# RWKV preparation: seven kinds of store to DRAM issued from POOL's queue instead of SP's and ACT's

## The chip, the core and the metric

The kernel runs on one core of a Trainium2 chip. The core has five engines, each working through its own list of instructions in order: PE (TensorE, matmuls), DVE (VectorE), ACT (ScalarE), POOL (GpSimd) and SP (SyncE). SP computes nothing: it only issues transfers. ACT and POOL can issue transfers too. An issue takes its place in the engine's own list, so an issue that has to wait holds up whatever stands behind it on that engine. The bytes are moved by 16 DMA engines, whichever engine issued the transfer.

The metric is device time in microseconds (us). Lower is better. Three runs of the kernel before gave a median of 2121.01 us.

## What is computed

The program is one block of a model over 512 latent tokens and 256 context tokens with 1024 channels: a token mixer with two branches (RWKV-7 and Mamba-2) and a mixture of 16 experts behind it. The change lies in the preparation of the RWKV branch, whose recurrence reads:

```python
def step(s, inp):
    r_t, w_t, k_t, v_t, kk_t, a_t = inp
    sa = jnp.einsum('bhvk,bhk->bhv', s, -kk_t)
    s = s * w_t[:, :, None, :] + sa[..., None] * (kk_t * a_t)[:, :, None, :] + v_t[..., None] * k_t[:, :, None, :]
    return s, (jnp.einsum('bhvk,bhk->bhv', s, r_t) if with_output else None)
s, ys = lax.scan(step, s0, seq, reverse=reverse)
```

It runs over 768 tokens, once forward and once backward, for 16 heads of 64 channels. All arithmetic is in float32.

## The kernel before

**The recurrence in chunks.** The 768 tokens are cut into 12 chunks of 64. Within a chunk the steps are solved at once, which needs products of the operands within the chunk and the inverse of a triangular 64x64 matrix. Only from chunk to chunk does a serial scan remain. All that the scan needs is made in a preparation stage, written to DRAM in the layout that the scan wants, and loaded again by `scan_load`.

**The preparation (`rw_all`).** It goes over 8 pairs of heads (p = 0 to 7) and two directions (d = 0 forward, 1 backward): 16 products, from about 100 to 640 us of the span. The pieces that matter here are these.

- `split_w` (L280 to L286) loads a weight block `wraw` of 512 KB on SP (L280), rounds it on ACT to `whi` (L283) and takes the rest on DVE to `wlo` (L286). PE projects the tokens with both (L311, L314). This input projection is the filler: between the small matmuls of the preparation PE works off its matmuls. `wraw` and `wlo` share three buffers.
- `rw_head` loads two small weights `lwr` (L609), rounds them on ACT (L612), and turns `v` into `VT` (L622, L623).
- `rw_elem` makes the operands `AR` and `BK` from exponentials; ACT evacuates its matmuls `ra`, `rac` into `s` and `a` (L660, L661).
- `rw_products` multiplies them on PE (`pab`, L735, L738), DVE masks the results into two tiles `X` (L741), and six stores per product put parts of X into `d1` (L748, four) and `d3` (L750, two): these are the operands of the inverses, 48 KB each in pieces of 128 bytes. Four more stores, from POOL, put X into `ALd` and `RBd` (L751, L752). Then PE transposes BK three times (`pbt`, L760), ACT copies each result to `BT` (L762; two buffers), and each BT is stored to `BTd` (L763, 256 KB). The third BT of a product needs the buffer of the first, so it waits until the first one's store has landed.
- `tri` loads `Ad` from `d1` (L778), builds 32x32 inverses on DVE (L783 to L805) and stores them twice, `Tf` and its transpose `Tt`, to `d2` (L809, L810).
- `tri2` loads them as `T11` and `TT` (L824, L821), joins them with `A21` (L826, from `d3`) into 64x64 inverses by PE (`px`, `py`, L835, L845) and ACT (L838, L848), and stores them to `TTd` (L852, two per pair). The last three pairs' `tri2` run beside the first scan.

**What sets the order.** PE's list stands as written in the code. DVE, ACT, POOL and SP are ordered by the framework's scheduler, which simulates the program when it is built. The same framework gives every transfer one of eight completion counters: the transfers of SP and ACT share eight (DMAHW0 to 7), those of POOL have another eight (DMASW0 to 7). In this program a transfer that takes a counter first waits until the transfer that had it before has landed.

**Queues before.** SP issues all loads, the stores to `d1`, `d3`, `d2` and `TTd`; ACT issues the stores to `BTd` and, at the end of the preparation, the loads of the first scan step (`scan_first`: `sAR`, `sBK`); POOL issues the stores to `ALd`, `RTd`, `RBd`, `VTd`, `bond`, `zd`.

Of the kernel before, what the change touches and what calls it, by code (L numbers as in the profile page):

```python
# [86 lines left out]
class Block:  # L87
# [629 lines left out]
    def rw_products(self, pool, ps, p, d, AR, BK, f, t2, last=False):  # L717

        nc = self.nc
        H = [slice(0, 64), slice(64, 128)]  # L720
        V = [H[1], H[0]]
        chunk = lambda s: s if d == 0 else (3 - s if s < 4 else 15 - s)
        al = AR.rearrange("q (g u) t -> q g (u t)", u=2)
        ALd, RTd, RBd = (x[p // 2][:, p % 2] for x in (self.ALd, self.RTd, self.RBd))
        for a in range(2):
            nc.gpsimd.dma_start(ALd[:, H[d], d, a].rearrange("g k t -> k g t"), al[H[a], 0:6])
            nc.gpsimd.dma_start(RTd[:, H[d], a].rearrange("g k t -> k g t"), al[H[a], 6:10])
        Xs = [pool.tile([128, 20, 64], F32, name="X", tag="X", bufs=2) for _ in range(2)]
        for u0, m in ((0, 1), (4, 2), (8, 2)):
            pa = [ps.tile([128, 4, m, 64], F32, name="pab", tag="ra") for _ in range(2)]  # L730
            for u in range(4):
                for a in range(2):
                    w = BK[H[a], chunk(u0 + u)].rearrange("p x t -> p (x t)")
                    if m > 1:
                        nc.tensor.matmul(pa[a][:, u], w, AR[H[a], u0 + u:u0 + u + 9:8, :], start=True, stop=True)  # L735
                    else:
                        for h in range(2):
                            nc.tensor.matmul(pa[a][H[h], u, 0], w[:, H[h]], AR[H[a], u, :], start=True, stop=True)  # L738
            for a, X in enumerate(Xs):
                o = X[:, 4:20].rearrange("p (x u) t -> p u x t", x=2)[:, u0 - 4:u0] if m > 1 else X[:, 0:4, None]  # L740
                nc.vector.tensor_mul(o, pa[a], self.mk[:, d, None, 0:m].to_broadcast([128, 4, m, 64]))  # L741
            f()
            f()
        for a, X in enumerate(Xs):
            xs = X.rearrange("q (g u) t -> q g (u t)", u=2)
            for b in range(2):
                q = 2 * d + b
                nc.sync.dma_start(self.d1[p % 3][:, 24 * q + 12 * a:24 * q + 12 * a + 12, :],  # L748
                                  X[32 * q:32 * q + 32, 0:12, 32 * b:32 * b + 32])
            nc.sync.dma_start(self.d3[p % 3][d, :, 12 * a:12 * a + 12], X[64 * d:64 * d + 32, 0:12, 32:64])  # L750
            nc.gpsimd.dma_start(ALd[:, V[d], d, a].rearrange("g k t -> k g t"), xs[V[d], 0:6])  # L751
            nc.gpsimd.dma_start(RBd[:, :, d, a].rearrange("g k t -> k g t"), xs[:, 6:10])  # L752
            next(t2, None)
        if last:
            self.first = self.scan_first()

        for g in range(3):
            pt = ps.tile([128, 4, 128], F32, name="pbt", tag="ra")
            for u in range(4):
                nc.tensor.transpose(pt[:, u], BK[:, chunk(4 * g + u)].rearrange("p x t -> p (x t)"), self.ident)  # L760
            BT = pool.tile([128, 4, 128], F32, name="BT", tag="BT", bufs=2)
            nc.scalar.activation(BT, pt, AF.Copy)  # L762
            nc.scalar.dma_start(self.BTd[p // 2][2 * g:2 * g + 2, p % 2, :, d].rearrange("g k u c -> k g (u c)"),  # L763
                                BT.rearrange("k (g u) c -> k g (u c)", u=2))
            f()
            next(t2, None)

    def tri(self, pool, p):

        nc = self.nc
        d1, d2 = self.d1[p % 3], self.d2[p % 2]
        T, Tf = self.T, self.Tf
        Ad = pool.tile([96, 3, 16, 16], F32, name="Ad", tag="Ad", bufs=2)
        lo, hi = slice(0, 16), slice(16, 32)
        for i, (x, y) in enumerate(((lo, lo), (hi, hi), (lo, hi))):
            nc.sync.dma_start(Ad[:, i], d1[x, :, y].rearrange("s u t -> u s t"))  # L778
        prod = lambda n: pool.tile([96, 512], F32, name="pr", tag="pr", bufs=PRB)[:, :n]
        for s in range(14, -1, -1):  # L780
            n, r = 15 - s, slice(s + 1, 16)
            prv = prod(2 * n * n).rearrange("p (h c t) -> p h c t", h=2, t=n)
            nc.vector.tensor_mul(prv, T[:, :, r, r], Ad[:, 0:2, s, r][:, :, None, :].to_broadcast([96, 2, n, n]))  # L783
            nc.vector.reduce_sum(T[:, :, r, s], prv, axis=AX.X)
            if s % 2 == 0:
                yield
        Tt = pool.tile([96, 32, 32], F32, name="Tt", tag="Tt", bufs=1)
        U, W = (Tt.rearrange("p a b -> p (a b)")[:, i:i + 256].rearrange("p (s x) -> p s x", x=16) for i in (0, 256))
        nc.scalar.activation(U, T[:, 0].rearrange("p x s -> p s x"), AF.Copy)
        nc.scalar.activation(Tf[:, 0:16, 0:16], T[:, 0], AF.Copy)  # L790
        nc.scalar.activation(Tf[:, 16:32, 16:32], T[:, 1], AF.Copy)
        for c in range(0, 16, 2):
            n = c + 2
            prv = prod(32 * n).rearrange("p (c s t) -> p c s t", c=2, s=16)
            nc.vector.tensor_mul(prv, T[:, 1, c:c + 2, 0:n][:, :, None, :].to_broadcast([96, 2, 16, n]),
                                 Ad[:, 2, :, 0:n][:, None].to_broadcast([96, 2, 16, n]))
            nc.vector.reduce_sum(W[:, c:c + 2], prv, axis=AX.X)
            if c % 4:
                yield
        for s in range(0, 16, 2):  # L800
            n = 16 - s
            prv = prod(32 * n).rearrange("p (c s x) -> p c s x", c=16, s=2)
            nc.vector.tensor_mul(prv, W[:, :, s:16][:, :, None, :].to_broadcast([96, 16, 2, n]),
                                 U[:, s:s + 2, s:16][:, None].to_broadcast([96, 16, 2, n]))
            nc.vector.reduce_sum(Tf[:, 16:32, s:s + 2], prv, axis=AX.X)  # L805
            if s % 4:
                yield
        nc.scalar.activation(Tt.rearrange("p c t -> p t c"), Tf, AF.Copy)
        nc.sync.dma_start(d2[:, 0], Tf)  # L809
        nc.sync.dma_start(d2[:, 1], Tt)  # L810

    def tri2(self, pool, ps, tag, p):

        nc = self.nc
        d2, d3 = self.d2[p % 2], self.d3[p % 3]
# [3 lines left out]
        for q in range(4):  # L819
            d, b = divmod(q, 2)  # L820
# [28 lines left out]
            if tag == "A":  # L849
                yield  # L850
        for a in range(2):
            nc.sync.dma_start(self.TTd[p // 2][:, p % 2, :, a].rearrange("g k t -> k g t"),  # L852
                              TT[:, 12 * a:12 * a + 12].rearrange("q (g u) t -> q g (u t)", u=2))
        yield

# [1267 lines left out]
```

## Time and profile before

| | us |
|---|---|
| median of three runs | 2121.01 |
| lowest and highest of the three | 2115.63, 2121.77 |
| the profiled execution | 2122.66 |
| its span (first to last instruction) | 2120.9 |
| PE busy in the span | 1865.1 |
| DVE busy in the span | 1245.5 |
| ACT busy in the span | 838.0 |
| POOL busy in the span | 256.3 |

The profile is of a fourth execution. The span is the time that its traced instructions cover; 1.8 us of the execution's own time lie around it. Busy time is summed over the whole span, which has stages with different limits, so a share of it says little on one stage: the preparation has to be read by itself.

### The profile page before, as it was taken

The page shows a single profiled execution, that of the slowest core. Times are in us where ns is not written, and L with a number is a line of the kernel's source. Part 1 is how long each engine was busy: PE and PEld are TensorE (multiplying, and loading weights), DVE is VectorE, ACT ScalarE, POOL GpSimd, SP SyncE. Part 2 cuts the span into 40 slices and gives each one's busy share as a digit, 9 for nine tenths or more (in the row PEclk, how much of TensorE's full clock was granted, in tenths as well). Part 3 has the DMA queues.
Part 4 walks back from the last instruction along what each step waited for, and adds up shares of the span by engine and source line. Part 5 has one row for each costly group of instructions (what it writes and reads, how often), then busy time and mean ns, then how long its engine had stood idle before and what let it go on. Part 6 is the DMA issues. An engine that isn't in the chain of part 4 may idle for free.

```text
span 2120.9 us, 34560 instructions
## 1 busy us (share of the span) xinstructions
PE 1865.1 (88%) x13683; PEld 1251.7 (59%) x13696; DVE 1245.5 (59%) x2240; ACT 838.0 (40%) x1344; POOL 256.3 (12%) x383
## 2 busy tenths in 40 slices
PE   5989788888778988998997997788999999999997
PEld 2867676676656755656675664467878444434332
DVE  4467888987878667545563888875355111324315
ACT  5445555555534344343535443354334112212113
POOL 1123333232320000000000000000001000000002
PEclk8989989999888999999998999789999999999999
DMA  6357686777779676976536334257766899999997
GB/s 240 90 129 173 154 201 180 184 169 192 182 196 241 213 244 196 288 238 188 176 119 207 122 125 136 100 185 259 256 219 255 335 409 409 409 409 409 403 409 290
DMA packets 388414, 495.13 MB, mean 233 GB/s; under 512 B 138521, under 2 KB 278031, under 8 KB 385179
## 3 DMA queue, kind: packets, MB, share of 16 engines
q1 hardware_dynamic: 349883, 407.33, 57.6%
q0 software_dynamic: 21504, 68.70, 11.1%
q10 hardware_dynamic: 16864, 16.88, 2.5%
q8 instruction: 108, 1.77, 0.3%
q14 instruction: 55, 0.45, 0.1%
HBM read 393.96 MB, written 97.98 MB: 232 GB/s over the span
## 4 chain that ended last, share of the span: by engine, by line
PE 50%; DVE 18%; DMA 17%; ACT 7%; issue 6%; SPq 1%; POOL 1%; ACTq 0%; POOLq 0%; DVEq 0%
PE pl L311 9%; PE ph L1713 6%; DMA ew<-in_exp_w_dram 5%; DMA wraw<-in_w_in_dram 5%; PE pch L901 4%; PE pye L1800 4%; PE mp L1361 4%; PE pc L314 3%; DVE wlo L286 2%; PE pl L1314 2%; PE sps L1180 1%; PE py L901 1%; DMA BTd<-BT 1%; PE adaps L167 1%; PE ph L1714 1%
## 5 line engine op out<-in xcount | busy, mean ns | idle before, releaser
L311 PE MATMUL pl<-hlH,whi 128*128 128x512 f32 x672 | 246.3, 446 | 15.7 <-ACT u L455 5.6
L311 PE MATMUL pl<-hlH,wlo 128*128 128x512 f32 x672 | 234.8, 426 | 0.0
L311 PE MATMUL pl<-hlL,whi 128*128 128x512 f32 x672 | 230.0, 422 | 0.0
L283 ACT ACTIVATE whi<-wraw 128x1024 fp32r<-128x1024 f32 x93 | 97.9, 1052 | 183.9 <-DMA wraw<-in_w_in_dram 83.5
L311 PEld LDWEIGHTS pl<-hlH,whi 128*128 128x128 f32 x672 | 133.9, 203 | 58.9 <-issue 14.5
L286 DVE TENSOR_TENSOR wlo<-wraw,whi 128x1024 fp32r<-128x1024 f32 x93 | 112.8, 1213 | 86.3 <-ACT whi L283 61.0
L1714 PE MATMUL ph<-ew,xe 128*64 128x512 f32 x336 | 148.8, 594 | 4.4 <-DMA ew<-in_exp_w_dram 4.4
L311 PEld LDWEIGHTS pl<-hlL,whi 128*128 128x128 f32 x672 | 128.5, 195 | 37.9 <-issue 11.4
L1713 PE MATMUL ph<-ew,xe 128*64 128x512 f32 x336 | 148.7, 594 | 0.0
L311 PEld LDWEIGHTS pl<-hlH,wlo 128*128 128x128 f32 x672 | 127.3, 195 | 35.6 <-issue 11.7
L314 PE MATMUL pc<-hcH,whi 128*128 128x256 f32 (+1 forms) x312 | 96.3, 312 | 7.2 <-ACT u L455 6.1
L1800 PE MATMUL pye<-ew,ewx 128*64 128x512 f32 x448 | 101.4, 597 | 0.0
L464 DVE SCALAR_TENSOR_TENSOR cacc<-u,cst,cacc 128x772 f32<-128x772 f32 (+1 forms) x96 | 93.4, 973 | 11.3 <-ACT cacc L460 9.8
L1828 DVE TENSOR_TENSOR macc<-macc,psc 128x512 f32<-128x512 f32 x56 | 36.8, 681 | 101.1 <-PE psc L1823 101.0
L314 PE MATMUL pc<-hcH,wlo 128*128 128x256 f32 (+1 forms) x312 | 94.2, 303 | 0.0
L314 PE MATMUL pc<-hcL,whi 128*128 128x256 f32 (+1 forms) x312 | 93.6, 304 | 0.0
L1720 ACT ACTIVATE ewx<-ph 128x512 f32<-128x512 f32 x30 | 17.9, 598 | 188.6 <-PE ph L1713 104.5
L1713 PEld LDWEIGHTS ph<-ew,xe 128*64 128x64 f32 x336 | 44.7, 137 | 78.9 <-issue 76.5
L1779 DVE TENSOR_TENSOR ewx<-ewx,pht 128x256 f32<-128x256 f32 x32 | 13.4, 419 | 108.3 <-ACT ewx L1778 108.0
L314 PEld LDWEIGHTS pc<-hcH,whi 128*128 128x128 f32 (+1 forms) x312 | 62.8, 201 | 15.6 <-ACT u L455 9.2
L1217 ACT ACTIVATE X<-selb,ncumT 128x128 f32<-128x128 f32 x128 | 36.4, 367 | 77.8 <-PE selb L1214 77.6
L314 PEld LDWEIGHTS pc<-hcL,whi 128*128 128x128 f32 (+1 forms) x312 | 60.7, 196 | 4.4 <-issue 2.1
(602 smaller groups left out, 4171.0 us busy)
## 6 DMA issues: line engine op xcount, KB each, us to landing
ew<-in_exp_w_dram SPq DMA_DIRECT2D x126, 1024.0 KB
ew<-in_exp_w_dram SPq DMA_DIRECT2D x90, 512.0 KB
wraw<-in_w_in_dram SPq DMA_DIRECT2D x83, 512.0 KB
adaw<-in_ada_w_dram SPq DMA_DIRECT2D x24, 1024.0 KB
cst<-in_exp_w_dram SPq DMA_DIRECT2D x14, 1024.0 KB
BTd<-BT ACTq DMA_DIRECT2D x48, 256.0 KB
sAL<-ALd SPq DMA_DIRECT2D x23, 512.0 KB
sBT<-BTd SPq DMA_DIRECT2D x23, 512.0 KB
```

The costliest lines, as they stand in the source:

```text
L283: pin(nc.scalar.activation(hi, raw, AF.Copy))
L286: self.lo.tensor_sub(lo, raw, hi.bitcast(F32))
L311: nc.tensor.matmul(pl[:n], w_[:, kt, :n], x[0][:, kt, :], **e)
L314: nc.tensor.matmul(pc[:n], w_[:, kt, :n], x[1][:, kt, :], **e)
L464: e.scalar_tensor_tensor(acc[:, s0:s0 + n0], u[:, s0 + k:s0 + k + n0], cw[:, b, k:k + 1], acc[:, s0:s0 + n0], op0=OP.mult, op1=OP.add)
L901: mm = lambda o, w, x, f=True, l=True: nc.tensor.matmul(o, w, x, start=f, stop=l, skip_group_check=True)
L1314: nc.tensor.matmul(po, w[x][:, k], self.ya[k][:, h], start=k + j == 0, stop=k == 7 and j == 2)
L1361: nc.tensor.matmul(po[ob], w[k][lo][:, ob * 128:ob * 128 + 128], yb[k][:, h], start=k + h + lo == 0, stop=k == 15 and lo == 1)
L1713: nc.tensor.matmul(ph[e][f][0:64], x, w1[j][:, fs], start=kt == 0, stop=kt == 7, skip_group_check=True)
L1714: nc.tensor.matmul(ph[e][f][64:128], x, w3[j][:, fs], start=kt == 0, stop=kt == 7, skip_group_check=True)
L1800: nc.tensor.matmul(py[64 * c:64 * c + 64], hd[e][:, kt], w2[j][:, 512 * c:512 * c + 512], start=kt == 0, stop=kt == 7, skip_group_check=True)
L1828: nc.vector.tensor_add(a, a, pc)
```

## The change

In `rw_products`, `tri` and `tri2` the stores named above are issued by `nc.gpsimd` in place of `nc.sync`, and those to `BTd` in place of `nc.scalar`:

```diff
             for b in range(2):
                 q = 2 * d + b
-                nc.sync.dma_start(self.d1[p % 3][:, 24 * q + 12 * a:24 * q + 12 * a + 12, :],
+                nc.gpsimd.dma_start(self.d1[p % 3][:, 24 * q + 12 * a:24 * q + 12 * a + 12, :],
                                   X[32 * q:32 * q + 32, 0:12, 32 * b:32 * b + 32])
-            nc.sync.dma_start(self.d3[p % 3][d, :, 12 * a:12 * a + 12], X[64 * d:64 * d + 32, 0:12, 32:64])
+            nc.gpsimd.dma_start(self.d3[p % 3][d, :, 12 * a:12 * a + 12], X[64 * d:64 * d + 32, 0:12, 32:64])
...
-            nc.scalar.dma_start(self.BTd[p // 2][2 * g:2 * g + 2, p % 2, :, d].rearrange("g k u c -> k g (u c)"),
+            nc.gpsimd.dma_start(self.BTd[p // 2][2 * g:2 * g + 2, p % 2, :, d].rearrange("g k u c -> k g (u c)"),
                                 BT.rearrange("k (g u) c -> k g (u c)", u=2))
...
-        nc.sync.dma_start(d2[:, 0], Tf)
-        nc.sync.dma_start(d2[:, 1], Tt)
+        nc.gpsimd.dma_start(d2[:, 0], Tf)
+        nc.gpsimd.dma_start(d2[:, 1], Tt)
...
-            nc.sync.dma_start(self.TTd[p // 2][:, p % 2, :, a].rearrange("g k t -> k g t"),
+            nc.gpsimd.dma_start(self.TTd[p // 2][:, p % 2, :, a].rearrange("g k t -> k g t"),
                               TT[:, 12 * a:12 * a + 12].rearrange("q (g u) t -> q g (u t)", u=2))
```

The stores, their bytes and the arithmetic are the same; 176 issues move (96 to d1 and d3, 48 to BTd, 16 to d2, 16 to TTd). PE's list does not change. The lists of the other four do, for the scheduler orders them anew. The place shown is the second product of pair p = 4 with the `tri2` of pair 2 beside it, at about 440 to 456 us of the profile before. In brackets stand the counters and engines that a row waits for. SP's list before:

```order
L748 DMA d_211<-X 32x12x32 [waits DMAHW0_49,DVE_49]
L748 DMA d_211<-X 32x12x32 [waits DMAHW1_49]
L750 DMA d_216<-X 32x12x32 [waits DMAHW2_49]
L280 DMA wraw<-in_w_in_dram 128x8x128 [waits DMAHW4_49,DMAHW3_49,DVE_49]
L852 DMA TTd_171<-TT 128x6x128 [waits Activation_49]
L826 DMA A_4837<-d_215 32x768 [waits DMAHW5_49,PE_49]
L778 DMA Ad<-d_211 96x16x16 [waits DMAHW6_49,DMAHW1_49,DMAHW0_49]
L852 DMA TTd_171<-TT 128x6x128 [waits DMAHW7_49,Activation_49]
```

SP's list of the change at the same place:

```order
L280 DMA wraw<-in_w_in_dram 128x8x128 [waits DMAHW3_49,DVE_49]
L826 DMA A_4837<-d_215 32x768 [waits PE_49,Activation_49]
L826 DMA A_4837<-d_215 32x768 [waits DMAHW4_49,DMASW6_49]
L778 DMA Ad<-d_211 96x16x16 [waits DMASW6_49,DMASW5_49,DMASW7_49,DMASW4_49,DMAHW5_49,DMASW3_49,DMASW2_49]
L778 DMA Ad<-d_211 96x16x16 [waits DMAHW6_49]
L778 DMA Ad<-d_211 96x16x16 [waits DMAHW7_49]
```

The stores of X and TT are gone from SP, so the load of `wraw` no longer stands behind them; the loads of `Ad` still wait for the stores to d1, now by POOL's counters. ACT's list before, at the same place:

```order
L762 ACTIVATE BT<-pbt 128x512 [waits PE_49]
L763 DMA BTd_168<-BT 128x2x256 [waits DMAHW0_49,Activation_49]
L789 ACTIVATE Tt<-T 96x256 [waits DMAHW5_49,DVE_49]
L790 ACTIVATE Tf<-T 96x16x16
L791 ACTIVATE Tf<-T 96x16x16
L762 ACTIVATE BT<-pbt 128x512 [waits DMAHW6_49,PE_49]
L763 DMA BTd_168<-BT 128x2x256 [waits DMAHW4_49,Activation_49]
L660 ACTIVATE s<-ra,cst 128x512 [waits PE_49]
L661 ACTIVATE s<-rac,cst 128x256 [waits PE_49]
L762 ACTIVATE BT<-pbt 128x512 [waits DMAHW0_49]
```

ACT's list of the change:

```order
L762 ACTIVATE BT<-pbt 128x512 [waits PE_49]
L762 ACTIVATE BT<-pbt 128x512 [waits DMASW7_49,PE_49]
L660 ACTIVATE s<-ra,cst 128x512 [waits PE_49,Activation_49]
L661 ACTIVATE s<-rac,cst 128x256 [waits PE_49]
L789 ACTIVATE Tt<-T 96x256 [waits DMASW0_49,DVE_49]
...
L326 ACTIVATE k<-pc,cst 128x256 [waits PE_49]
L762 ACTIVATE BT<-pbt 128x512 [waits DMASW3_49]
```

The issues of the stores are gone from ACT, and here the third BT has moved back behind 13 other instructions. Over all 16 products of the change, six have nothing, or only `nkk` (L617), between the second and the third BT; in the other ten at least four instructions stand there. POOL's list of the change, which before held only the rows of L751, L752 and L481:

```order
L748 DMA d_211<-X 32x12x32 [waits DMASW3_49,DVE_49]
L748 DMA d_211<-X 32x12x32 [waits DMASW4_49]
L750 DMA d_216<-X 32x12x32 [waits DMASW5_49]
L751 DMA ALd_156<-X 64x6x128 [waits DMASW6_49]
L752 DMA RBd_164<-X 128x4x128 [waits DMASW7_49]
L481 DMA zd_123<-zg 128x512 [waits DMASW0_49,DVE_49]
L852 DMA TTd_171<-TT 128x6x128 [waits DMAHW1_49,DMAHW6_49,DMAHW0_49,DMAHW7_49,DMASW1_49,Activation_49]
L852 DMA TTd_171<-TT 128x6x128 [waits DMASW2_49,Activation_49]
L763 DMA BTd_168<-BT 128x2x256 [waits DMASW3_49,Activation_49]
L763 DMA BTd_168<-BT 128x2x256 [waits DMASW4_49,Activation_49]
```

So for each of the two X tiles five stores now stand in a row on POOL, and the stores of BT come behind all ten. Every row waits for a counter of POOL's own eight.

## Rows read from the trace of the kernel before

**Rows 1.** Stretch, length, busy PE, PEld, DVE, ACT, POOL, clock, DMA share, GB/s.

```profile
200.00:600.00 400.00, 334.34 (x3008) 267.46 (x3007) 337.88 (x668) 212.40 (x318) 120.36 (x180) 0.91 0.74 181
```

**Rows 2.** Chain that ended last, 100 to 640 us, shares by line (shortened by the tool).

```profile
by line: DMA wraw<-in_w_in_dram 13.7%; issue 12.9%; PE pl L311 5.5%; DMA BTd<-BT 4.1%; DVE wlo L286 4.0%; DVE X L741 3.4%; DVE T L784 2.9%; DVE pr L783 2.8%; DMA TTd<-TT 2.6%; DMA lwr<-in_rw_a_dram 2.5%; DMA sBK<-ALd 2.2%; SPq L609 2.0%; DV
```

**Rows 3.** Waits of ACT, 100 to 640 us: total, times, longest.

```profile
ACT whi L283 <- DMA wraw<-in_w_in_dram: 69.5, 18, 8.3
...
ACT BT L762 <- DMA BTd<-BT: 21.7, 8, 5.6
...
ACT s L660 <- DMA TTd<-TT: 8.2, 2, 4.9
```

**Rows 4.** Line L789 in a timeline of ACT, 508 to 526 us.

```profile
522.90 0.63 ACT L789 ACTIVATE Tt<-T 96x256 f32<-96x256 f32 x1 [5.43 <-DMA TTd<-TT]
```

**Rows 5.** Timelines at 449 to 456 us: ACT, then PE; idle before in brackets.

```profile
449.67 0.58 ACT L762 ACTIVATE BT<-pbt 128x512 f32<-128x512 f32 x1
454.69 0.37 ACTq L763 DMA_DIRECT2D BTd<-BT  x1
455.10 0.69 ACT L660 ACTIVATE s<-ra,cst 128x512 f32<-128x512 f32 x1 [4.85 <-DMA TTd<-TT]
...
455.84 0.39 PE L656 MATMUL rac<-low,lwh 128*128 128x256 f32 x1 [3.49 <-ACT s L660]
```

**Rows 6.** Chain at 447 us: start, us, what.

```profile
447.33 7.28 DMA TTd<-TT
```

**Rows 7.** Timelines at 241 to 257 us: DVE, SP, ACT.

```profile
241.05 1.21 DVE L286 TENSOR_TENSOR wlo<-wraw,whi 128x1024 fp32r<-128x1024 f32 x1
...
244.59 1.74 SPq L750 DMA_DIRECT2D d<-X  x1
246.43 3.21 SPq L280 DMA_DIRECT2D wraw<-in_w_in_dram  x1
...
256.12 1.06 ACT L283 ACTIVATE whi<-wraw 128x1024 fp32r<-128x1024 f32 x1 [8.32 <-DMA wraw<-in_w_in_dram]
```

**Rows 8.** Timelines at the end of the preparation: SP, then DVE.

```profile
606.82 7.13 SPq L748 DMA_DIRECT2D d<-X  x2
...
616.32 0.42 DVE L741 TENSOR_TENSOR X<-pab,cst 128x256 f32<-128x256 f32 x1 [4.26 <-DMA d<-X]
618.80 0.42 DVE L741 TENSOR_TENSOR X<-pab,cst 128x256 f32<-128x256 f32 x1 [2.06 <-DMA d<-X]
```

**Rows 9.** POOL's issues by line, 100 to 640 us: count, busy, mean ns, idle before.

```profile
L752 POOL DMA_DIRECT2D RBd<-X x32 | 24.7, 772 | 0.0
L751 POOL DMA_DIRECT2D ALd<-X x32 | 21.6, 675 | 62.3 <-DVE X L741 51.0 <-DVE Tf L805 6.9 <-DVE pr L783 4.2
```

**Rows 10.** First products of pairs 5 and 6: chain, SP and ACT timelines.

```profile
472.99 3.92 DMA BTd<-BT
...
486.03 1.06 ACT L283 ACTIVATE whi<-wraw 128x1024 fp32r<-128x1024 f32 x1 [5.32 <-DMA wraw<-in_w_in_dram]
...
540.64 0.84 SPq L748 DMA_DIRECT2D d<-X  x2
...
542.62 5.76 DMA BTd<-BT
...
553.64 1.06 ACT L283 ACTIVATE whi<-wraw 128x1024 fp32r<-128x1024 f32 x1 [2.24 <-DMA wraw<-in_w_in_dram]
```

**Rows 11.** DMA queues of the whole span (q1 SP, q0 POOL, q10 ACT): packets, MB, share.

```profile
q1 hardware_dynamic: 349883, 407.33, 57.6%
q0 software_dynamic: 21504, 68.70, 11.1%
q10 hardware_dynamic: 16864, 16.88, 2.5%
```

**Rows 12.** POOL's issues, median us to landing: whole span, then 238 to 256 us.

```profile
RBd<-X POOLq DMA_DIRECT2D x32, 256.0 KB, 5.4
...
RBd<-X POOLq DMA_DIRECT2D x2, 256.0 KB, 7.0
```

## The prediction

> **What bounds the kernel now.** The change touches only the preparation, so I read that stage first, by busy time, then the chain that ended last, then the waits, and last the timelines around the waits that the chain passes.
>
> From 200 to 600 us PE is busy for 334.34 of 400 us and DVE for 337.88, ACT for 212.40 and POOL for 120.36 [rows 1]. So no engine is full. PE idles 65.7 us and DVE 62.1 us there, and a change of queues can win back some of that and nothing more. The chain says what fills the idle time: 13.7% of the stretch of 540 us is spent in loads of `wraw`, 4.1% in stores of BT and 2.6% in stores of TT [rows 2]: 74, 22 and 14 us. That a store stands on a path at all is the point to look at, because nothing computes with its result soon.
>
> The waits show where the stores hold an engine. ACT waits 69.5 us for `wraw`, 21.7 us for the stores of BT (eight times) and 8.2 us at L660 for stores of TT [rows 3], and 5.43 us more at L789 [rows 4]. The last two are odd, since L660 does not read TT. At 449.67 ACT copies a BT, and then ACT's own issue of that BT's store comes only at 454.69, because its completion counter is still held by a store of TT that SP issued and that took 7.28 us [rows 5, 6]. So `s` at L660 comes 4.85 us late, and PE, whose next matmul needs the PSUM buffer, idles 3.49 us [rows 5]. PE lost 3.49 of 4.85, a share of 0.72. I use that share below to turn a wait of ACT or DVE into time of the stage. It comes from one place; the range has to carry that.
>
> **The change part by part.**
>
> *A. Stores of TT and BT leave the counters that ACT and SP share.* ACT issues no store of BT any more, so its wait for a counter goes: 8.2 + 5.43 = 13.6 us of ACT [rows 3, 4], at 0.72 it is 9.8 us. What would be late next at L660 is PE's own `ra`, and that had ended, since PE stood waiting for ACT [rows 5]. Bounds: nothing and 13.6 us. I take 9.8.
>
> *B. Loads no longer stand behind the stores of X.* At 241 us `wlo` ended at 241.05 + 1.21 = 242.26 and gave its buffer back, but SP was issuing stores of X, and the next `wraw` went out at 246.43. `whi` waited 8.32 us for it [rows 7]. The load could go 4.2 us sooner. I count this place once, 4.2 x 0.72 = 3.0 us, since at most other places SP waits for the buffer and not for its own stores. Bounds: nothing, and 4.2 us at each of the seven second products that a next pair follows, 29 us.
>
> *C. The last stores of X.* In the last pair SP could not place them: two issues took from 606.82 to 613.95, behind the scan's first loads, which ACT issues and which have 2.2% of the chain [rows 2]. DVE needs the X buffers and stands for 4.26 and 2.06 us [rows 8], together 6.3 us. On POOL the stores need none of these counters and go out when X is ready. 6.3 x 0.72 = 4.6 us. Bounds: nothing and 6.3 us.
>
> *D. POOL's queue gets longer.* An issue there takes 0.675 us for `ALd` and 0.772 us for `RBd` [rows 9]. No store of X from POOL to `d1` stands in the trace, so I price it by `ALd`, which has as many pieces per transfer. Ten stores now stand ahead of a product's first BT: 8 x 0.675 + 2 x 0.772 = 6.9 us after X is ready. Before, ACT issued that store 542.62 - 540.64 = 2.0 us after the first store of X [rows 10]. So it leaves 4.9 us later and lands 4.9 us later, and the third BT, which needs its buffer, waits that much longer. The 176 issues as a whole, some 0.7 us each, are 123 us of POOL over the stage's 540 us, where it is busy for 120.36 of 400 us [rows 1], so it has room.
>
> In ten of the 16 products the new order puts at least four other instructions of ACT between the second and third BT: I price these at nothing. The work that hides the wait there is `s`, `a`, `whi` and the exponentials; if that cover is gone, it is 4.9 us each. In six products, which are first products of a pair, the third BT follows directly, with `v`, `r` and the next `whi` queued behind it on ACT, and PE's transposes of `v` behind those. 6 x 4.9 = 29.4 us more wait. But at these places the load of `wraw` stands behind the stores of X and then `whi` waits once more, 5.32 and 2.24 us at the two shown, 3.8 us in the mean [rows 10]. With the load issued earlier that second wait lies beside the first. So 6 x (4.9 - 3.8) = 6.6 us are left, x 0.72 = 4.8 us lost. Bounds: nothing, and 29.4 us.
>
> *E. The rest.* The stores to `d2` go from SP to POOL; their loads T11 and TT still wait on SP for the same DVE and ACT work, so I price it at nothing, hidden by DVE's work on the next inverse; uncovered it is one POOL issue, 0.7 us for each of 8 pairs, 6 us. ACT's 48 issues go; ACT has 187.6 us idle in 400 [rows 1], so nothing for that either.
>
> *The sum.* -9.8 - 3.0 - 4.6 + 4.8 = -12.6 us. From the profiled execution's 2122.66 us that is 2110.1. The median of the runs is 1.65 us below the profiled execution, so I predict **2108 us** for the median, 0.6% less.
>
> One rule speaks against this. The queue rows first: q0 moved 68.70 MB in 21504 packets and q1 407.33 MB in 349883 [rows 11], 3195 and 1164 bytes each; and in the burst at 238 to 256 us a POOL store landed after 7.0 us where the median is 5.4 [rows 12]. The Trainium skill ("DMA: Bandwidth & Descriptors", "Queues, rings and completion order") says that a DMA engine takes turns between its queues packet by packet, draining a whole packet before it switches. By that rule a load beside a POOL burst gets 1164 of 4359 bytes, about a quarter, and the sum would turn; the trace shows the unequal packets but not the turns. I keep the sum without it, since the same bytes crowd the same burst before, and give it a place among the rivals.
>
> **The rivals.**
>
> *No change.* PE and DVE are both over 80% busy and in order, so the freed waits are filled by the next in line. If half of A, B and C arrives, it is -8.7 + 4.8 = -3.9 us, 2117 us. For it: ACT's largest wait, for `wraw`, is mostly not due to the stores. Against: the 3.49 us that PE lost are shown. The Trainium skill ("DMA: Bandwidth & Descriptors", "Issuing engines are not separate DMA queues") says that transfers of all issuing engines share the same DMA engines and that spreading the issues saves only their issue time. By it this rival would be the likeliest; the 4.85 us of ACT are not issue time, and the trace does not agree there.
>
> *Slower: the third BT.* If the load's wait does not fold into the BT's, D costs 29.4 x 0.72 = 21.2 us, and the sum is 21.2 - 17.4 = +3.8 us, 2125; with landings of 7.0 in place of 5.4 us, 6 x 1.6 x 0.72 = 6.9 us more, 2132. It decides from a net cost of 17.4 / 0.72 / 6 = 4.0 us for each of the six. For it: the stores of BT are on the chain at just these products [rows 10]. Against: the scheduler has moved the third BT back in ten others.
>
> *Slower: loads starved by POOL's burst.* POOL's 68.70 MB cost 11.1% of the span, 3.4 us per MB [rows 11]. A product's moved stores are 6 x 48 + 3 x 256 KB, 1.08 MB, 3.7 us. If half of ACT's 18 waits for `wraw` [rows 3] grow by that, it is 9 x 3.7 x 0.72 = 24 us, so +11 us, 2132; with all of them, 2156.
>
> *More gain.* If B holds at all seven products, 6 more times 3.0 us, it is -30.6 us, 2090.
>
> **How the numbers follow.** About 0.3% (6.4 us) is what a measurement of this kernel can tell from no change. My chances: the forecast 0.49 (its own range 2094 to 2114), more gain 0.07, no change 0.21, the third BT 0.16, starved loads 0.07. The range of 2088 to 2133 us holds the forecast, no change, the BT case and the nearer half of the two outer cases, 0.85 or so. Faster by over 0.3%: 0.56; within: 0.21; slower: 0.23.
>
> **What would show it.** A: no wait of L660 or L789 for a store of TT. B: `wraw` issued within 1 us of the `wlo` that frees its buffer, and ACT's 69.5 us for `wraw` down by 20 us or more. C: no stall of X on a store at 612 to 619 us. D: ACT's 21.7 us for the stores of BT up, to 40 us or so, in the six first products. The prediction is wrong if that wait passes 50 us while the one for `wraw` stays, if loads take longer from issue to landing, or if POOL's issues themselves begin to wait on its eight counters so that `E` or `AR` comes late.

## The result and the profile after

The median of four runs of the changed kernel is 2092.24 us (2087.82 to 2098.13), of four runs of the kernel before beside it 2121.39 us: a ratio of 0.9862 with a 95% interval of 0.9843 to 0.9881, 29 us or 1.4% less. Faster was the forecast, and the time lies inside the range, but the gain is more than twice the 12.6 us of the sum. It lies next to the rival that stood at 2090 us.

The profiled execution after took 2089.19 us with a span of 2087.4 us. PE's list is the same in both kernels, so the same matmul can be looked up in both traces. The first matmul of the scan that reads `SV` (L901) shows what was gained up to there. Line view of L901, with the header that gives the span (before, then after):

```profile
core 0 of [0], span 2120.9 us
...
L901 PE MATMUL pch<-SV,sAL x736: 222/222/370, 657.0 to 1098.5; 128*64 128x64 f32 x184
```

```profile
core 0 of [0], span 2087.4 us
...
L901 PE MATMUL pch<-SV,sAL x736: 222/222/369, 624.2 to 1066.1; 128*64 128x64 f32 x184
```

It starts 657.0 - 624.2 = 32.8 us sooner, and the span is 33.5 us shorter: nearly all of the gain is made ahead of it. The window of 200 to 600 us, and the chain from 100 to 640 us, of after:

```profile
200.00:600.00 400.00, 349.11 (x3122) 277.13 (x3120) 362.76 (x739) 219.29 (x328) 231.17 (x338) 0.92 0.76 197
```

```profile
by line: issue 9.5%; PE pl L311 9.1%; DMA wraw<-in_w_in_dram 7.1%; DVE wlo L286 5.0%; DVE X L741 4.9%; DVE pr L803 3.1%; DVE Tf L805 3.0%; PE pc L314 2.8%; DMA BTd<-BT 2.6%; DVE BK L695 2.3%; DVE pr L783 1.8%; DVE Tt L797 1.8%; DVE T L784 1
```

Against [rows 1] DVE's idle time fell from 62.1 to 37.2 us and PE's from 65.7 to 50.9 us. Against [rows 2] the loads of `wraw` fell from 13.7% to 7.1% of the chain, 74 to 38 us, and the stores of TT are gone from it. The waits of ACT, DVE and SP in the same stretch of 100 to 640 us (total, times, longest), after:

```profile
ACT whi L283 <- DMA wraw<-in_w_in_dram: 57.8, 20, 9.2
...
ACT BT L762 <- DMA BTd<-BT: 11.4, 4, 6.2
...
DVE wlo L286 <- ACT whi L283: 17.0, 9, 4.1
DVE s L665 <- ACT s L661: 11.6, 6, 4.1
...
SPq L280 <- DVE wlo L286: 162.0, 33, 10.2
```

The rows of DVE and SP before, which the prediction does not show:

```profile
DVE s L665 <- ACT s L661: 33.1, 9, 8.4
DVE wlo L286 <- ACT whi L283: 31.2, 9, 10.8
...
DVE X L741 <- DMA d<-X: 8.3, 3, 4.3
...
SPq L280 <- DVE wlo L286: 109.4, 22, 12.9
SPq L748 <- DVE X L741: 51.0, 14, 6.9
...
SPq L810 <- ACT Tt L808: 19.3, 5, 7.2
```

DVE lost 33.1 us to `s`, 31.2 us to `whi` and 8.3 us to X's stores; after it loses 11.6, 17.0 and nothing. SP used to stand 51.0 us at its stores of X, waiting for DVE's X, and 19.3 us at L810 waiting for ACT's `Tt`, with loads behind it. After the change none of its waits is for the data of a store. Its loads of `Ad` wait longer for the stores of X (L778, 8.7 to 23.8 us), but its largest wait is at L280, ready for the buffer: that this one grew, 109.4 to 162.0 us, costs nothing, for it is SP that is early. The load at the place of [rows 7] shows it (DVE, SP):

```profile
246.78 1.21 DVE L286 TENSOR_TENSOR wlo<-wraw,whi 128x1024 fp32r<-128x1024 f32 x1
...
248.06 0.39 SPq L280 DMA_DIRECT2D wraw<-in_w_in_dram  x1
```

`wlo` ends at 247.99 and the load is issued 0.07 us later, where it came 4.17 us later before. I worked this out for all loads of the stretch from the timelines of SP and DVE: the end of each issue of `wraw` less the end of the `wlo` ahead of it. It is 1.58 us in the mean of 39 loads before and 0.51 us in 41 after. Where nothing holds SP it is 0.4 to 0.5 us; what goes beyond 0.6 us sums to 42 us before and to 3 us after. Below I call that sum the **lag**.

### The profile page after: what moved, and what is told of

Read it like the earlier page. It is cut to its first block, busy times and chain, and to the rows that moved or that the text cites. A ratio compares the mean times of both kernels' runs of the same rounds, so it can differ in the third digit from the quotient of the medians.

```text
span 2087.4 us, 34615 instructions
## 1 busy us (share of the span) xinstructions
PE 1859.0 (89%) x13696; PEld 1249.1 (60%) x13696; DVE 1245.2 (60%) x2240; ACT 839.0 (40%) x1344; POOL 380.1 (18%) x559
## 4 chain that ended last, share of the span: by engine, by line
PE 51%; DVE 21%; DMA 14%; ACT 6%; issue 5%; POOL 1%; SPq 0%; DVEq 0%; POOLq 0%; ACTq 0%
PE pl L311 10%; PE ph L1713 6%; DMA ew<-in_exp_w_dram 5%; PE pch L901 5%; PE pye L1800 4%; PE pc L314 4%; PE mp L1361 4%; DMA wraw<-in_w_in_dram 3%; DVE wlo L286 2%; PE pl L1314 2%; DVE X L741 1%; PE py L901 1%; PE sps L1180 1%; PE adaps L167 1%; PE ph L1714 1%
## 5 line engine op out<-in xcount | busy, mean ns | idle before, releaser
L311 PEld LDWEIGHTS pl<-hlL,whi 128*128 128x128 f32 x672 | 129.4, 196 | 38.1 <-issue 11.4
L1779 DVE TENSOR_TENSOR ewx<-ewx,pht 128x256 f32<-128x256 f32 x32 | 13.4, 418 | 108.1 <-ACT ewx L1778 107.9
```

The source lines that it names most:

```text
L311: nc.tensor.matmul(pl[:n], w_[:, kt, :n], x[0][:, kt, :], **e)
```

## Experiments

All ratios, with their 95% intervals in brackets, are to runs of the kernel before on the same chip in the same batch, where it took 2125 to 2127 us; a gain in us is the ratio by that median. The changed kernel itself ran only in the first batch, so a difference between it and e1 to e18 is one of two ratios. Theories 1 to 3 were there from the start. Theory 4 was formed after e4, theory 5 after e8 and theory 6 after e12. "Order" is the order of DVE's and ACT's instructions.

### One part at a time: e1 to e4

Each moves one kind of store, the others stay.

```diff
 # e1: L748 and L750      e2: L763 (from nc.scalar)      e3: L852      e4: L809 and L810
-            nc.sync.dma_start(
+            nc.gpsimd.dma_start(
```

> Only the 96 stores of X to d1 and d3 go to POOL; BT stays on ACT, the stores to d2 and TTd stay on SP. The prediction's terms B and C would give -7.6 us. Theory 1 (the gain of 29 us is loads that no longer stand behind stores on SP): -18 us or more, with ACT's wait for wraw and the chain's share of wraw (13.7% before, 7.1% after the whole change) well down. Theory 2 (ACT freed of the stores of BT and of their counters): -8 us or less, and the chain's share of wraw stays above 10%. Theory 3 (the scheduler's new order of DVE and ACT is what counts, the queues are not): the time may go either way by up to 10 us, and the four single parts don't add up to 29 us.

> Only the 48 stores of BT go from ACT to POOL; X, d2 and TTd stay on SP. The prediction's term A (ACT issues no store, so it waits for no counter of a TT store) would give -9.8 us, and term D nothing here, for no store of X stands ahead of BT on POOL. Theory 1: -5 us at most. Theory 2: -15 us or more, with s at L660 waiting for no store of TT. Theory 3: either way by up to 10 us.

> Only the 16 stores of TT go from SP to POOL; BT stays on ACT, X and d2 on SP. ACT's waits of 13.6 us for stores of TT must go, since these hold none of its counters any more. By term A -9.8 us. Theory 1: SP has 16 stores of 192 KB that wait for ACT's L848 less ahead of its loads, so -3 to -12 us, with wraw issued sooner after them. Theory 2: -9.8 us with no change of wraw. Theory 3: either way by up to 10 us.

> Only the 16 stores of Tf and Tt to d2 go from SP to POOL. The prediction's term E gives nothing. Theory 1: these stores wait on SP for DVE's last reduction and ACT's L808, with wraw behind them, so -2 to -10 us. Theory 2: nothing, within 4 us. Theory 3: either way by up to 10 us.

Measured: X 0.9937 [0.9919, 0.9955], -13.4 us; BT 0.9961 [0.9948, 0.9973], -8.3 us; TT 0.9995 [0.9980, 1.0010], nothing; d2 1.0024 [1.0009, 1.0039], +5 us. Together -18 us, not -29. e1 lies outside the ranges of all three theories, e2 to e4 only inside the wide one of theory 3. In e1 the lag is down to 9 us, but ACT's wait for `wraw` went up to 88.5 us, since the loads took longer to land: from the end of the issue to `whi` 6.2 us in the mean against 5.0 before (see the last section). TT alone takes the wait for a counter away, as it should, and gets nothing for it. The place of [rows 5] in e3:

```profile
455.47 0.60 ACT L762 ACTIVATE BT<-pbt 128x512 f32<-128x512 f32 x1 [5.77 <-DMA BTd<-BT]
455.96 0.68 ACT L660 ACTIVATE s<-ra,cst 128x512 f32<-128x512 f32 x1
```

Where the counter of a TT store no longer holds ACT ahead of `s`, the third BT does, waiting for its buffer: one wait lay behind the other. Over the whole stage DVE's wait for `s` is 32.8 us in e3, where it was 33.1 before.

### Exchanging single elements, the scheduler free: e5 to e8

e5 traces the third BT of a second product after the next `s` and holds it there (`issue_after` is an edge of issue order only); e6 does the reverse in the changed kernel.

```diff
 # e5, in rw_elem
+            act = nc.scalar.activation(o[:, :CTX], pc, AF.Tanh, bias=bias, scale=0.5); self.after_s(act, p, d, i)
...
+            with self.tc.issue_after(act.ins):
+                self.pend()
 # e6, in rw_elem
+            with self.tc.issue_after(self.third) if d == 1 and i == 0 and p > 0 else ExitStack():
 # e7, the changed kernel with L763 on nc.scalar;  e8, with L748 and L750 on nc.sync
```

> The kernel before with every store on its old queue; only ACT's order is changed: the third BT of a pair's second product is traced after s of the next product and held behind L661 on ACT, seven times. In the trace of before DVE waits 33.1 us at L665 for s, and 21.6 us of it stand behind a third BT that waits for its buffer, or behind a store of BT that waits for a counter held by a store of TT. Theory 4 (ACT's place of the third BT ahead of s is the larger half of the gain, whichever queue the stores are on): -10 to -22 us, with L665's wait for s down to 12 us or so. Theory 1 (loads behind stores on SP): within 5 us, for the loads stand as before. If both hold, the rest of the 29 us is the stores of X.

> The changed kernel with every store on POOL; only ACT's order is changed: s of the next product is held behind the third BT, seven times, as the scheduler had it before the change. Theory 4: +10 to +22 us against the changed kernel (so -7 to -19 us against before), with L665's wait for s back to 25 to 40 us. Theory 1: within 5 us of the changed kernel, -24 to -34 us against before.

> The change without its stores of BT: those stay on ACT, all others go to POOL. Theory 1: -20 us or more against before. Theory 4: the third BT stands ahead of s again, so -10 to -16 us (X alone gave -13.4 us, TT and d2 alone nothing or worse), and ACT's wait for the buffer of BT stays at 20 us or more.

> The change without its stores of X: those stay on SP, the stores of BT, d2 and TT go to POOL. Theory 1: -10 us or less, as BT alone gave -8.3 us. Theory 4: -15 to -22 us, with no third BT ahead of s. In both DVE waits 4 to 9 us for X's buffer again at the end of the stage.

Measured: e5 1.0029 [1.0015, 1.0042]; e6 1.0245 [1.0223, 1.0267], 52 us above before; e7 0.9987 [0.9967, 1.0006]; e8 0.9960 [0.9942, 0.9978]. e5 is a miss for theory 4: DVE's wait at L665 stayed at 32.9 us. e6 is a miss for theories 1 and 4. But around the forced place the scheduler had set everything else anew, so neither e5 nor e6 says what the place alone is worth. In e6 the loss is in waits that no theory named:

```profile
DVE pr L783 <- DMA Ad<-d: 63.6, 6, 14.0
...
PE pab L738 <- ACT BT L762: 48.6, 6, 11.8
```

Why these grew in e6 stays open. With the scheduler free, neither BT nor X can be left out: without BT (e7) the gain is 3 us, which its interval does not tell from nothing, and without X (e8) 9 us. Theory 4 misses both, theory 1 the first. DVE's wait for X's buffer, expected at 4 to 9 us in both, is 1.7 and 0.6 us.

### Queues and order apart: e9 to e12

The instructions of both kernels have the same names, so the order of one can be laid on the other: an edge of issue order between each two neighbours, on DVE and on ACT. The lists of both engines over the preparation then agree row for row with the kernel that the order is from. SP's and POOL's lists are still the scheduler's: in e12 SP's loads come in the order of before, in e10, e13 and e15 to e17 they come in a new one. The changed kernel with its own order held, which would show what the holding costs by itself, was not run.

```diff
+ORDER = ["84 731 68 73 85 86 75 74 81 76 ...", "..."]
+def pin_order(tc):
+    by = {i.name: i for i in tc.nc.cur_bb.bb.instructions}
+    for row in ORDER:
+        row = ["I-" + n for n in row.split()]
+        for a, b in zip(row, row[1:]):
+            tc.add_manual_dep(by[b], a, mybir.DependencyInfo(mybir.DependencyClass.NoSync, mybir.DependencyReason.DATA), reason="order")
```

> Every store is on its old queue, but the 1163 instructions of DVE and the 625 of ACT in the preparation are held to the order that they have in the changed kernel. Theory 3 (the new order of DVE and ACT is what gave the 29 us): -20 to -29 us. Theory 5 (the queues themselves: a load of wraw goes out as soon as its buffer is free, and nothing of ACT waits for a store's counter): 0 to -8 us, or slower, for SP still holds the loads behind the stores of X and ACT now meets its issues of BT's stores at other places. If both are needed together, -8 to -20 us.

> Every moved store is on POOL as in the changed kernel, but DVE and ACT are held to the order that they have before the change (1163 and 625 instructions). Theory 3: within 6 us of before. Theory 5: -15 us or more. In both, wraw goes out within 0.6 us of the wlo that frees its buffer, and the third BT stands ahead of s as before, so that DVE's wait at L665 stays at 15 us or more.

> Only the stores of X go to POOL, and DVE and ACT are held to the order of before, so that the queue is the only thing changed. In the traces the end of wraw's issue lags the end of the wlo ahead of it by 1.58 us in the mean of 39 loads before, 0.51 us after the whole change, 0.67 us with X alone on POOL in the scheduler's own order. Theory 5: -12 to -25 us, from loads that are 1 us earlier 39 times, less what loads lose by landing beside POOL's stores. Theory 3: within 5 us of before, and the -13.4 us of X alone came from its order.

> Only the stores of BT go to POOL, and DVE and ACT are held to the order of before. ACT issues no store, so it waits for no counter of a TT store (13.6 us before), but the third BT stands ahead of s as before and waits for its buffer. Theory 5: -3 to -12 us, with L665's wait down by the 13 us that stood behind counters. Theory 3: within 5 us of before.

Measured: the new order on the old queues (e9) 1.0018 [1.0005, 1.0030]; the new queues in the old order (e10) 1.0028 [1.0017, 1.0039]; X alone in the old order (e11) 0.9988 [0.9975, 1.0001]; BT alone in the old order (e12) 0.9918 [0.9903, 0.9934], -17 us. So neither the new queues as a whole nor the new order gives anything by itself, and both together give 29 us. BT's queue alone does give something in the old order, where all moved stores together give nothing. How its 17 us come about is not shown. Theories 3 and 5 both fall as stated, theory 3 by e9 and theory 5 by e10 and e11; e12 fits neither. In e9 the lag stays at 41 us and SP stands 62.2 us at its stores of X, as before the change. The waits of ACT in e10 say what went wrong there:

```profile
ACT BT L762 <- DMA BTd<-BT: 61.0, 12, 10.1
ACT whi L283 <- DMA wraw<-in_w_in_dram: 42.2, 15, 4.4
```

The loads are better than in the changed kernel (42.2 against 57.8 us; the lag is 14 us, of which 11 at one load that waited for PE), but ACT waits 61.0 us for stores of BT, against 21.7 us in [rows 3]. In e12, with the same order and no moved store but BT's on POOL, it is 36.6 us. With the stores of X ahead of them on POOL, the stores of BT land later: a product's first one 7.1 us after the end of its copy in e10 and 5.3 us in e12, in the mean of 16. The time goes into the place in POOL's list (the issue ends 3.4 and 1.6 us after the copy), not into the transfer (median 4.2 and 4.9 us from issue to landing). In the old order the third BT stands ahead of the next product's `s` in three of the first seven pairs, and behind it but ahead of `a`, or of the second half of `a`, in the other four: DVE's wait for `s` is 40.2 us in e10.

### The one element of the order: e13 to e16

e13 and e14 take the table of the old order and move seven numbers of ACT's row, each a third BT, to behind the second L661 that follows. e15 and e16 hold the new order and put X back on SP, or BT back on ACT.

```diff
 # ACT's row of ORDER by line, first of seven places (e13, e14)
-762 762 660 661 283 660 661
+762 660 661 283 660 661 762
```

> As e10 (all moved stores on POOL, DVE and ACT held to the order of before), but with the third BT of the second product of the first seven pairs moved on ACT from ahead of, or just behind, the next s to behind the s and a of the next product (behind the second L661 that follows). Theory 6 (the stores of X ahead of BT on POOL make the third BT late, and this costs only while s stands behind it): -15 to -29 us against before, with ACT's wait for a BT store down from 61.0 to 15 to 35 us. Rival (many places of the order matter, the third BT's is one of them): within 8 us of e10, that is 0 to +8 us against before.

> The same seven moves of the third BT on ACT, with every store on its old queue and the rest of DVE's and ACT's order as before. Theory 6: within 8 us of before, for X's stores still hold SP's loads; DVE's wait at L665 goes down by some 8 us at most, for the waits for a counter held by a TT store stay. Rival (the place alone is the gain): -10 us or more.

> The changed kernel with DVE and ACT held to its own order, and the 96 stores of X back on SP. Theory 6: the loads of wraw lag wlo by 1.5 us in the mean again, 40 us in all, and DVE waits for X at the end of the stage: -3 to -14 us against before, so that B and C together are worth 15 to 26 us of the 29. Rival (X's stores hardly matter): -20 us or more.

> The changed kernel with DVE and ACT held to its own order, and the 48 stores of BT back on ACT. Theory 6: the loads stay early, and the third BT is behind s, but ACT issues 48 stores again at 0.4 us or more each and the loads land beside two queues of stores instead of one (5.0 us from issue to whi before, 4.9 after, 6.0 in e7): -8 to -20 us against before. Rival (BT's queue hardly matters in the new order): -22 us or more.

Measured: e13 0.9923 [0.9896, 0.9950]; e14 0.9980 [0.9964, 0.9997]; e15 1.0018 [1.0001, 1.0035]; e16 0.9903 [0.9874, 0.9932]. Moving seven instructions of 1788 takes e10's +6 us to -16 us, 22 of the 35 us between e10 and the changed kernel; the scheduler's lists for SP and POOL changed with it, and the other 13 us are not traced. On the old queues the same seven moves give 4 us. ACT's waits in e13:

```profile
ACT whi L283 <- DMA wraw<-in_w_in_dram: 46.5, 17, 4.6
...
ACT BT L762 <- DMA BTd<-BT: 21.8, 7, 8.7
```

The loads stayed as good as in e10, and the wait for BT went from 61.0 to 21.8 us, so theory 6 holds in e13 and e14. It forecast -3 to -14 us for e15, where the loss of X's queue took the whole gain; e16 lies at the edge between it and its rival. In e15, with X back on SP in the new order, SP's and ACT's waits are the old ones (lag 33 us):

```profile
SPq L748 <- DVE X L741: 56.0, 15, 6.9
...
ACT whi L283 <- DMA wraw<-in_w_in_dram: 90.2, 19, 9.4
```

So in the new order X's stores alone are worth 0.9862 to 1.0018, 33 us: more than expected. In the old order they were worth 3 us (e11). BT's are worth 0.9862 to 0.9903, 9 us, give or take 7 by the two intervals, which overlap.

### The rest: e17 and e18

Stores to `d2` and `TTd` back on SP; e17 in the changed kernel's order, e18 in the scheduler's own.

> X and BT on POOL, the 32 stores of d2 and TTd back on SP, DVE and ACT held to the order of the changed kernel. Term E (d2 is worth nothing) and TT's 16 stores now hold none of ACT's counters that matter: -24 to -31 us against before, RBd landing in 4.4 to 4.8 us as in the changed kernel. Rival (any store ahead of a load on SP costs, whichever it is): d2 and TT wait on SP for DVE and ACT with wraw behind them, wraw's lag after wlo back to 0.9 us or more in the mean, and -14 to -22 us.

> The same stores on POOL as in e17, with the order left to the scheduler. If its order puts the third BT behind s as in the changed kernel, as e17 within 6 us; if it does not, as e10, 0 to +8 us against before.

Measured: e17 0.9937 [0.9919, 0.9956]; e18 0.9917 [0.9901, 0.9934]. The 32 stores are worth 16 us beside the others in that order and 12 us with the scheduler's own, though alone they were worth nothing (e3, e4). e17 misses its own forecast. Its rival nearly named the price but not the mechanism: the lag is 6 us, so few loads were late. The scheduler's order in e18 has the third BT behind `s` in the first seven pairs, and e18 is within 6 us of e17, as expected. What grew is ACT's wait for `wraw`, 66.6 against 57.8 us, and SP stands at these stores again. For L809 and L810 in e17:

```profile
SPq L809 <- DVE T L784: 16.6, 2, 14.6
...
SPq L809 <- DVE Tf L805: 15.2, 3, 10.9
SPq L810 <- ACT Tt L808: 15.1, 6, 5.4
```

How these 47 us on SP become 16 us of time is not shown. No version that was run beats the changed kernel.

## Why the gain was forecast too small, point by point

**A, counters: right in kind.** No wait of L660 or L789 for a store of TT is left. Its mechanism is real on DVE too: at three of the nine places where DVE waited for `s` before, ACT's last wait was for a TT store. But e3 shows that this wait covered another one, and its price can't be separated from BT's. BT moved alone in the old order gave 17 us (e12), against 9.8 for A, and these are more than A's waits.

**B, loads behind X's stores: the step that failed.** "I count this place once", "since at most other places SP waits for the buffer and not for its own stores". The lag says 42 us over the stretch before, more than 1 us at 15 of 39 loads, and 3 us after: not one place of 4.2 us. The prediction left out SP's own waits: 51.0 us at L748 for DVE's X, ahead of loads. In the new order X's stores are worth 33 us (e15), where B and C had 7.6 us. ACT's 69.5 us for `wraw` were the wrong witness: they went down by 11.7 us, not by the 20 that I named, while the lag fell by 39 us.

**C, X's buffers at the end: right.** DVE's 8.3 us for stores of X are gone. It is inside the 33 us.

**D, the third BT: right mechanism, wrong sign of its term.** The +4.8 us did not come: ACT's wait for stores of BT fell from 21.7 to 11.4 us, and 6.2 of these are the very last BT. The term took ten stores to stand ahead of a product's first BT on POOL, as in the second product that the lists show. In the six first products that it charged, the scheduler put the store of the first BT ahead of all ten: its issue ends 1.0 us after the copy (1.1 us in the mean before), and not 4.9 us later. The first product of pair 6 after (POOL):

```profile
511.72 0.72 POOL L763 DMA_DIRECT2D BTd<-BT  x1 [3.37 <-ACT BT L762]
513.10 1.26 POOL L748 DMA_DIRECT2D d<-X  x2 [0.65 <-DVE X L741]
```

I priced the ten products in which the scheduler moved the third BT back at nothing, but in the old order they had cost something already. The first of them, before (ACT, DVE):

```profile
188.52 0.60 ACT L762 ACTIVATE BT<-pbt 128x512 f32<-128x512 f32 x1 [5.58 <-DMA BTd<-BT]
189.14 0.37 ACTq L763 DMA_DIRECT2D BTd<-BT  x1
189.56 0.69 ACT L660 ACTIVATE s<-ra,cst 128x512 f32<-128x512 f32 x1 [0.44 <-ACT BT L762]
...
190.64 0.56 DVE L665 TENSOR_SCALAR s<-s 128x768 f32<-128x768 f32 x1 [8.44 <-ACT s L661]
```

The same `s` after, with the third BT behind it:

```profile
177.45 1.07 ACT L762 ACTIVATE BT<-pbt 128x512 f32<-128x512 f32 x2
178.61 0.69 ACT L660 ACTIVATE s<-ra,cst 128x512 f32<-128x512 f32 x1
...
180.06 0.75 DVE L665 TENSOR_SCALAR s<-s 128x768 f32<-128x768 f32 x1 [1.66 <-ACT s L661]
```

DVE's wait there went from 8.44 to 1.66 us. That the mechanism itself is real is shown by e10, where the order leaves the third BT uncovered: +6 us, between the +3.8 and +10.7 us that the rival of the third BT forecast. The 21.2 us that this rival charged for D are near the 22 us of e13 by chance: the moves of e13 are at the second products of a pair, where `s` follows, and not at the first ones, where I looked.

**E, the rest: wrong beside the others.** Nothing was priced; TT and d2 are worth 12 to 16 us once X and BT have moved, and nothing alone.

**The rivals.** "More gain" was the nearest. Its mechanism (B at more places) is there in the lag, but its number is in part luck: B at all places gives 3 us by itself (e11), and 33 us only with the rest. "No change" is what either half of the change does: queues or order. By the rule of the Trainium skill ("DMA: Bandwidth & Descriptors", "Issuing engines are not separate DMA queues") that only issue time is saved, 29 us are too much: loads no longer stand behind stores that wait for DVE (51.0 us at L748), and this trace does not agree with the rule. Loads starved by POOL's burst did not come: the loads lost least with all stores on POOL.

**The sum itself.** It treated the terms as independent. They are not: a wait that is removed uncovers the next one in the same queue (e3), X's gain needs the third BT out of the way (e11, e10, e13), and the single parts, -13, -8, 0 and +5 us, do not add up to -29.

## What to carry to other kernels

Read the issuing engine's own waits: a store that waits for its data, in the same engine's list as loads, delays each load behind it, and the waits of the computing engines do not name it. Where a scheduler orders the program anew, hold its order fixed, the issuing engines' lists too if they can be held, and change one thing at a time; here queues and order gave +6 and +4 us singly and -29 us together. An instruction that waits for a buffer belongs behind the work that others wait for, not ahead of it.

## What the runs showed of the hardware

In this kernel, stores of X and BT on one queue crowded the loads less than the same stores on two. POOL's issues by median time to landing (KB each, us) for the changed kernel, then e16, which has BT's stores on ACT and the same order of DVE and ACT (SP's and POOL's lists came out anew), then e1:

```profile
RBd<-X POOLq DMA_DIRECT2D x32, 256.0 KB, 4.5
...
ALd<-AR POOLq DMA_DIRECT2D x32, 192.0 KB, 4.0
```

```profile
RBd<-X POOLq DMA_DIRECT2D x32, 256.0 KB, 5.8
...
ALd<-AR POOLq DMA_DIRECT2D x32, 192.0 KB, 3.9
```

```profile
RBd<-X POOLq DMA_DIRECT2D x32, 256.0 KB, 6.3
...
ALd<-AR POOLq DMA_DIRECT2D x32, 192.0 KB, 3.8
```

`RBd`, which goes out in the burst of X and BT, lands after 4.5 us with BT on POOL and after 5.8 and 6.3 us with BT on ACT; `ALd<-AR`, outside the burst, stays at 3.8 to 4.0 us. The loads go the same way: from the end of `wraw`'s issue to `whi`, where `whi` waited for it, 4.9 us in the mean after (20 loads) and 6.0 us in e16 (21 loads), worked out from the timelines of SP and ACT; ACT's wait for `wraw` is 57.8 and 87.4 us. So part of BT's 9 us in e16 may be the loads'. The other runs go with it: the four kernels with every moved store on POOL (the changed one, e6, e10, e13) have 4.4 to 4.5 us for `RBd` and 4.5 to 4.9 us for the loads, the four with X on POOL and BT on ACT (e1, e7, e11, e16) 5.6 to 6.5 and 6.0 to 6.2 us. The kernel before has 5.0 us (18 loads) with stores on three queues, so the count of queues is not the whole of it. The Trainium skill ("DMA: Bandwidth & Descriptors", "Queues, rings and completion order") says that a DMA engine takes turns between the queues that have work; a second queue of stores would then take a turn from the loads. e16 agrees with it, but no run here shows the turns, and whether it is these or POOL's spacing of its issues stays open.
